# Row maxima of two dense attentions: one 128-row matmul per piece, or pairs of 64-row matmuls on the halves of the array

## The chip, the cores and the metric

One Trainium2 chip, and of it one core. The metric is the device time of one execution of the whole kernel, in microseconds (us); lower is better.

## The reference

Two transformer layers over 2048 latent tokens (width 1024) and a prefix of 256 context tokens. Each layer runs a modulated RMS norm, one input projection, two attentions, a gate, one output projection and a residual. The change touches the two *dense* attentions, mixer A of layer 0 (8 query heads, 2 key heads) and mixer C of layer 1 (4 heads, two maps each):

```python
def gqa_attend(q5, k, v):
    sc = jnp.einsum('bqkgd,bskd->bkgqs', q5, k).astype(jnp.float32) * SCALE
    p = jax.nn.softmax(sc, axis=-1).astype(v.dtype)
    return jnp.einsum('bkgqs,bskd->bqkgd', p, v)

def diff_attend(q, k, v, lam):
    sc = jnp.einsum('bqhmd,bkhmd->bhmqk', q, k).astype(jnp.float32) * SCALE
    p = jax.nn.softmax(sc, axis=-1)
    a = (p[:, :, 0] - lam * p[:, :, 1]).astype(v.dtype)
    return jnp.einsum('bhqk,bkhe->bqhe', a, v)
```

Heads are 64 wide, and all 2048 + 256 = 2304 keys are seen by each latent query. A softmax needs some number near the row's maximum, which is taken off before the exponential; any such number gives the same quotient.

## The kernel before

Every fp32 operand of an attention is kept as two fp16 halves, high and low. In DRAM, `qk` holds for each head 128 rows: rows 0 to 63 are the high half of the 64 channels, rows 64 to 127 the low half. `dense_kv` (line 1129) loads for a head `KH`, 128 rows by 2304 keys, with the high half of the keys *twice* (rows 0 to 63 and again 64 to 127), and `KL`, 65 rows, the low half and a row of constants.

`r_phase` (line 807) runs a dense attention. A unit is one head (or one map of one head) for 256 queries; each of the two attentions has 64 units. For the unit two ahead of the current one, the generator `r_front` (line 743) does the following:

- loads `Qt` (128 rows: high over low half of the queries) and `Q2` (65 rows: the high half, and a row still to be filled), on SyncE's queue;
- for each of the two halves of the queries (`t`), and for each of five pieces of the keys (four of 512, one of 256), one matmul into a PSUM tile `pM` and one VectorE reduction of it to a maximum (`mx`, line 759). With `Qt` stationary and `KH` moving, the 128 rows add up (high + low half of q) times the high half of k;
- takes the maximum over the five (`m`), writes its negative into `Z`, and brings it by a small matmul (`pM<-idh,Z`) into the last row of `Q2`.

Per unit these are 8 matmuls of 512 columns and 2 of 256, so 1024 and 256 in all. There are two `pM` buffers. For the current unit, `r_scores` (line 773) computes the scores transposed (`pS`), exponentiates on ScalarE (`Pm`), splits into `H` (ScalarE) and `L` (GpSimd), and `r_values` (line 793) multiplies by the values into `pO`. The output projection (`out_pair`, line 867; tiles `yT`, `wo`, `pX`) is fed in between as filler.

The generator is stepped a few times after each of the unit's five score groups: `for _ in range((3, 3, 2, 2, 3)[g])` (line 846). That is only the order in which the program is written down. The tile framework then simulates the program and sets each engine's order by it, so what stands next to what on TensorE follows from that scheduler and not from the source alone. All matmuls and weight loads go through the helper on line 82.

The projections ahead of an attention (`pmm<-wk,hT`) are matmuls of 256 columns. Two other matmuls matter below as a measure. `mod_cols` (line 144) issues matmuls with a stationary operand of 2 columns (`pO<-macc,sel`), which the program addresses as 128 rows by 32 columns of the array, and transposes of 2 rows (line 175, `pO<-idf,m`), addressed as 32 rows by 128 columns. All other matmuls of the attention stages and projections are addressed as the whole array, 128 by 128.

Of the kernel before, what the change touches and what calls it, by code (L numbers as in the profile page):

```python
# [8 lines left out]
F32 = mybir.dt.float32  # L9
F16 = mybir.dt.float16  # L10
AF = mybir.ActivationFunctionType
ALU = mybir.AluOpType
AX = mybir.AxisListType
# [3 lines left out]
P = 128  # L17
# [18 lines left out]
class Build:  # L36
# [424 lines left out]
    def t_block(self, Q, qs, segs, parts, tiles, nadd, add, esc, out, sink=None):  # L461
# [30 lines left out]
        yield  # L492
        Q2 = self.ap.tile([65, P], F16, name="Q2", bufs=3)
        nc.gpsimd.tensor_copy(out=Q2[0:64], in_=Q[0:64, qs])
        pz = self.ptr.tile([P, 512], F32, name="ptr")
        self.mm(pz[0:65, 0:P], Z, self.idh)
        nc.vector.tensor_copy(out=Q2[64:65], in_=pz[64:65, 0:P])
        yield
        Sb = self.ap.tile([P, 896], F32, name="Sb", bufs=self.sbufs)
        a, c0 = nadd * P, 0  # L500
        for part in (tiles[:min(nadd, 4)], tiles[min(nadd, 4):]):
# [3 lines left out]
            for j, (kh, kl, v) in enumerate(part):  # L505
                o = T[:, j * P:(j + 1) * P]
                self.mm(o, kh, Q[:, qs], True, False)
                self.mm(o, kl, Q2, False, True)
            w = len(part) * P
# [233 lines left out]
    def r_front(self, l, unit, qb, KH):  # L743

        nc = self.nc
        Qt = self.qp.tile([P, 256], F16, name="Qt")
        Q2 = self.qp.tile([65, 256], F16, name="Q2")
        nc.sync.dma_start(out=Qt, in_=self.qk[l][unit, :, qb * 256:(qb + 1) * 256])
        nc.sync.dma_start(out=Q2[0:64], in_=self.qk[l][unit, 0:64, qb * 256:(qb + 1) * 256])
        self.Qcur = (Qt, Q2)  # L750
        yield
        Zs = []
        for t in range(2):
            mx = self.smf.tile([P, 5], F32, name="mx")
            for j in range(5):
                c, n = j * 512, min(512, NTOK - j * 512)
                ps = self.pM.tile([P, 512], F32, name="pM")
                self.mm(ps[:, :n], Qt[:, t * P:(t + 1) * P], KH[:, c:c + n])
                nc.vector.tensor_reduce(out=mx[:, j:j + 1], in_=ps[:, :n], op=ALU.max, axis=AX.X)  # L759
                yield  # L760
            m = self.smf.tile([P, 1], F32, name="m")
            nc.vector.tensor_reduce(out=m, in_=mx, op=ALU.max, axis=AX.X)
            Z = self.Z[self.zi % 4]
            self.zi += 1
            nc.vector.tensor_scalar(out=Z[:, 64:65], in0=m, scalar1=-1.0 / T15, scalar2=None, op0=ALU.mult)
            Zs.append(Z)
        yield
        pz = self.pM.tile([P, 512], F32, name="pM")
        for t in range(2):
            self.mm(pz[0:65, t * P:(t + 1) * P], Zs[t], self.idh)  # L770
        nc.vector.tensor_copy(out=Q2[64:65], in_=pz[64:65, 0:256])
# [35 lines left out]
    def r_phase(self, units, front, back, finish, d, fillers):  # L807


        pend, Qs = [], []  # L810
        self.late, self.pxi = False, 0
        def first():
            e = self.early if d == 128 else self.earlyA
            return self.tc.high_priority(offset=e) if e else ExitStack()
        with first():
            for u in units[:2]:
                for _ in front(u):
                    pass
                Qs.append(self.Qcur)
        credit = [0.0] * len(fillers)  # L820

        def values():
            u, g, args, V = pend.pop(0)
            if g == 0:
                o = self.pO.tile([P, 512], F32, name="pO")
                self.Ov = o.rearrange("p (t x) -> p t x", t=2)
            self.r_values(*args, self.Ov, V, d)
            if g == 4:
                with self.tc.high_priority(offset=self.boost):
                    finish(u, self.Ov)  # L830
        for n, u in enumerate(units):
            Q = Qs.pop(0)
            f = iter(())
            self.late = n + 2 >= len(units)
            if n + 2 < len(units):
                f = front(units[n + 2])
                next(f)
                Qs.append(self.Qcur)
            KH, KL, V, esc = back(u)
            for g in range(5):  # L840
                if n == 0:
                    with first():
                        args = self.r_scores(g, Q, KH, KL, esc)
                else:
                    args = self.r_scores(g, Q, KH, KL, esc)
                for _ in range((3, 3, 2, 2, 3)[g]):
                    next(f, None)
                for i, (filler, rate) in enumerate(fillers):
                    credit[i] += rate(n)
                    while credit[i] >= 1.0:  # L850
                        credit[i] -= 1.0
                        filler.step()
                if len(pend) == self.lag:
                    values()
                pend.append((u, g, args, V))
        while pend:
            values()
# [731 lines left out]
```

## Time and profile before

| | us |
|---|---|
| median of 3 runs (lowest, highest) | 3759.36 (3756.82, 3761.03) |
| the profiled execution | 3757.87 |
| its span in the profile | 3756.1 |

The profiled execution is 1.5 us under the median, and 1.8 us longer than its span. Busy time by engine: TensorE (PE) 3596.3 us, VectorE (DVE) 2622.6, ScalarE (ACT) 2453.2, GpSimd (POOL) 2331.9.

How to read what follows: a view of the trace gives for each instruction its start and its duration. Matmuls are pipelined, so a matmul's duration (start to the last result) is longer than the distance to the next one's start. What the array gives to a matmul is that distance. A shape such as `128*128 128x256` reads: stationary operand of 128 rows by 128 columns, moving operand of 128 rows by 256 columns.

### The profile page before, as it was taken

The page shows a single profiled execution, that of the slowest core. Times are in us where ns is not written, and L with a number is a line of the kernel's source. Part 1 is how long each engine was busy: PE and PEld are TensorE (multiplying, and loading weights), DVE is VectorE, ACT ScalarE, POOL GpSimd, SP SyncE. Part 2 cuts the span into 40 slices and gives each one's busy share as a digit, 9 for nine tenths or more (in the row PEclk, how much of TensorE's full clock was granted, in tenths as well). Part 3 has the DMA queues.
Part 4 walks back from the last instruction along what each step waited for, and adds up shares of the span by engine and source line. Part 5 has one row for each costly group of instructions (what it writes and reads, how often), then busy time and mean ns, then how long its engine had stood idle before and what let it go on. Part 6 is the DMA issues. An engine that isn't in the chain of part 4 may idle for free. (4 is left out here: it accounts for less than half of the span.)

```text
span 3756.1 us, 104444 instructions
## 1 busy us (share of the span) xinstructions
PE 3596.3 (96%) x43146; PEld 2986.7 (80%) x43146; DVE 2622.6 (70%) x6646; ACT 2453.2 (65%) x4155; POOL 2331.9 (62%) x1822
## 2 busy tenths in 40 slices
PE   8889999989989999999989999999989999999998
PEld 5668988878976777777768999899878888888775
DVE  5757779898567666667666988767565656665666
ACT  5315656556668887778864666666567777776665
POOL 3204456666458888888864445435358878877785
PEclk9989999999999999999999999999999999999999
DMA  7673332223261111111133221312351211111322
GB/s 236 181 200 86 86 88 80 69 73 92 72 201 54 36 65 32 49 48 49 38 121 104 66 61 58 92 58 75 112 173 30 79 47 56 62 37 52 106 92 103
DMA packets 331972, 321.08 MB, mean 85 GB/s; under 512 B 84262, under 2 KB 283750, under 8 KB 330982
## 3 DMA queue, kind: packets, MB, share of 16 engines
q1 hardware_dynamic: 331494, 314.40, 27.7%
q8 instruction: 337, 5.52, 0.6%
q14 instruction: 141, 1.16, 0.1%
HBM read 207.43 MB, written 106.90 MB: 84 GB/s over the span
## 5 line engine op out<-in xcount | busy, mean ns | idle before, releaser
L790 POOL TENSOR_TENSOR L<-Pm,H 128x1024 f16<-128x1024 f32 (+1 forms) x640 | 1240.9, 1959 | 284.2 <-ACT H L788 207.3
L82 PE MATMUL pmm<-wk,hT 128*128 128x256 f16 x10848 | 1356.9, 275 | 21.1 <-POOL hT L277 7.2
L82 PEld LDWEIGHTS <-hT 128*128 128x128 f16 x10848 | 1026.9, 98 | 164.1 <-issue 21.8
L759 DVE TENSOR_REDUCE mx<-pM 128x1 f32<-128x512 f32 (+1 forms) x1280 | 785.7, 633 | 505.6 <-PE pM L82 496.4
L82 PE MATMUL pO<-V,H 128*128 128x65 f16 (+3 forms) x9216 | 781.0, 206 | 3.4 <-DVE ya L1267 1.8
L82 PEld LDWEIGHTS <-H 128*128 128x128 f16 x9216 | 641.5, 98 | 97.5 <-DVE ya L1267 5.2
L82 PE MATMUL pO<-V,L 128*128 128x65 f16 (+1 forms) x4608 | 707.9, 209 | 6.2 <-POOL L L790 5.8
L521 POOL TENSOR_TENSOR Pl<-Sb,Ph 128x640 f16<-128x640 f32 (+4 forms) x288 | 435.8, 1513 | 433.4 <-ACT Ph L520 260.6
L788 ACT CAST H<-Pm 128x1024 f16<-128x1024 f32 (+1 forms) x640 | 602.7, 959 | 11.8 <-PE pO L82 1.9
L82 PE MATMUL pS<-Qt,KH 128*128 128x256 f16 x2304 | 557.4, 273 | 6.2 <-ACT Pm L785 3.8
L82 PE MATMUL pS<-Q,KL 65*128 65x256 f16 x2304 | 548.1, 273 | 0.0
L82 PEld LDWEIGHTS <-L 128*128 128x128 f16 x4608 | 441.3, 97 | 51.0 <-POOL L L790 10.9
L82 PE MATMUL pM<-KH,Qt 128*128 128x512 f16 (+1 forms) x1280 | 446.5, 358 | 19.5 <-DVE mx L759 14.0
L785 ACT ACTIVATE Pm<-pS,esc_c 128x1024 f32<-128x1024 f32 (+1 forms) x320 | 323.0, 1025 | 203.8 <-PE pS L82 186.1
L82 PEld LDWEIGHTS <-KL 65*128 65x128 f16 x3824 | 371.5, 98 | 69.3 <-issue 15.7
L785 ACT ACTIVATE Pm<-pS,esc_a 128x1024 f32<-128x1024 f32 (+1 forms) x320 | 324.2, 1026 | 147.0 <-PE pS L82 109.6
L82 PE MATMUL pX<-wo,yT 128*128 128x512 f16 x1488 | 390.5, 381 | 2.0 <-ACT yT L897 1.3
L82 PEld LDWEIGHTS <-KH 128*128 128x128 f16 x2304 | 226.5, 98 | 60.7 <-issue 8.3
L82 PEld LDWEIGHTS <-yT 128*128 128x128 f16 x1632 | 154.3, 98 | 135.0 <-ACT yT L897 5.7
L520 ACT CAST Ph<-Sb 128x640 f16<-128x640 f32 (+4 forms) x288 | 220.0, 764 | 43.2 <-PE pO L82 35.0
L82 PE MATMUL pT<-Q,K 128*128 128x128 f16 x1520 | 230.7, 220 | 9.9 <-ACT Sb L516 5.0
L82 PE MATMUL pT<-Q,KL 65*128 65x128 f16 x1520 | 211.5, 220 | 0.0
(299 smaller groups left out, 5758.8 us busy)
## 6 DMA issues: line engine op xcount, KB each, us to landing
qk<-qkst SPq DMA_DIRECT2D x104, 256.0 KB, 2.3
wmod<-w_mod SPq DMA_DIRECT2D x24, 1024.0 KB, 9.1
xo<-x SPq DMA_DIRECT2D x48, 512.0 KB, 3.5
xt<-x SPq DMA_DIRECT2D x34, 512.0 KB, 4.8
G<-zz SPq DMA_DIRECT2D x68, 256.0 KB, 2.5
x<-xo SPq DMA_DIRECT2D x34, 512.0 KB, 3.3
wst<-w_in_even SPq DMA_DIRECT2D x13, 1024.0 KB, 5.5
wst<-w_in_odd SPq DMA_DIRECT2D x13, 1024.0 KB, 5.4
```

What stands on the lines that cost most here:

```text
L82: return self.nc.tensor.matmul(out=out, lhsT=l, rhs=r, start=s, stop=e, skip_group_check=skip)
L520: nc.scalar.copy(out=H[:, :n * P], in_=Sb[:, :n * P])
L521: nc.gpsimd.tensor_tensor(out=L[:, :n * P], in0=Sb[:, :n * P], in1=H[:, :n * P], op=ALU.subtract)
L759: nc.vector.tensor_reduce(out=mx[:, j:j + 1], in_=ps[:, :n], op=ALU.max, axis=AX.X)
L785: nc.scalar.activation(out=Pm[:, :n], in_=S[:, :n], func=AF.Exp, scale=esc[0], bias=LNP)
L788: nc.scalar.copy(out=H[:, :n], in_=Pm[:, :n])
L790: eng.tensor_tensor(out=L[:, :n], in0=Pm[:, :n], in1=H[:, :n], op=ALU.subtract)
```

## The change

The maxima are taken over the product of the high halves alone, 64 rows instead of 128. Two pieces form a pair: the first uses `Qt[0:64]` with `KH[0:64]`, the second uses a further tile `Qd`, into whose rows 64 to 127 the high half of the queries is loaded once more, with `KH[64:128]`. The two are thus addressed to the upper and lower 64 rows of the array (64 by 128 each) and written into the two `pM` buffers; then come the two reductions. The number of matmuls, their columns and the reductions stay; each unit gets one more DMA. The generator has fewer steps, so it is stepped (1, 1, 1, 1, 2) times.

```diff
@@ r_front
         Qt = self.qp.tile([P, 256], F16, name="Qt")
         Q2 = self.qp.tile([65, 256], F16, name="Q2")
+        Qd = self.qp.tile([P, 256], F16, name="Qd")
         nc.sync.dma_start(out=Qt, in_=self.qk[l][unit, :, qb * 256:(qb + 1) * 256])
+        nc.sync.dma_start(out=Qd[64:128], in_=self.qk[l][unit, 0:64, qb * 256:(qb + 1) * 256])
         nc.sync.dma_start(out=Q2[0:64], in_=self.qk[l][unit, 0:64, qb * 256:(qb + 1) * 256])
         self.Qcur = (Qt, Q2)
         yield
         Zs = []
-        for t in range(2):
-            mx = self.smf.tile([P, 5], F32, name="mx")
-            for j in range(5):
+        mxs = [self.smf.tile([P, 5], F32, name="mx") for t in range(2)]
+        for pair in (((0, 0), (0, 1)), ((0, 2), (0, 3)), ((1, 0), (1, 1)), ((1, 2), (1, 3)), ((0, 4), (1, 4))):
+            pss = []
+            for r, (t, j) in enumerate(pair):
                 c, n = j * 512, min(512, NTOK - j * 512)
                 ps = self.pM.tile([P, 512], F32, name="pM")
-                self.mm(ps[:, :n], Qt[:, t * P:(t + 1) * P], KH[:, c:c + n])
-                nc.vector.tensor_reduce(out=mx[:, j:j + 1], in_=ps[:, :n], op=ALU.max, axis=AX.X)
+                rows = slice(64 * r, 64 * r + 64)
+                self.mm(ps[:, :n], (Qt, Qd)[r][rows, t * P:(t + 1) * P], KH[rows, c:c + n])
+                pss.append((ps, n))
+            for (t, j), (ps, n) in zip(pair, pss):
+                nc.vector.tensor_reduce(out=mxs[t][:, j:j + 1], in_=ps[:, :n], op=ALU.max, axis=AX.X)
+            if pair[1] != (1, 4):
                 yield
+        for t in range(2):
+            mx = mxs[t]
             m = self.smf.tile([P, 1], F32, name="m")
...
@@ r_phase
-                for _ in range((3, 3, 2, 2, 3)[g]):
+                for _ in range((1, 1, 1, 1, 2)[g]):
                     next(f, None)
```

Where the scheduler puts these matmuls on TensorE, before, in the attention of layer 1 (`pO<-V,H` and `pO<-V,L` are the value products of the unit under way):

```order
L82 MATMUL pO<-V,H 128x129
L82 LDWEIGHTS Qt
L82 MATMUL pM<-KH_58635,Qt 128x512
L82 LDWEIGHTS H
L82 MATMUL pO<-V,H 128x128
L82 LDWEIGHTS L
L82 MATMUL pO<-V,L 128x129
L82 LDWEIGHTS Qt
L82 MATMUL pM<-KH_58635,Qt 128x512
L82 LDWEIGHTS H
L82 MATMUL pO<-V,H 128x129
```

Maxima and value products alternate, all of them over the whole array. TensorE's order with the change, in the same attention, one pair (`Qt` upper, `Qd` lower half):

```order
L82 LDWEIGHTS Qt
L82 MATMUL pM<-KH_62883,Qt 128x256
L82 LDWEIGHTS H
L82 MATMUL pO<-V,H 128x128
L82 LDWEIGHTS L
L82 MATMUL pO<-V,L 128x129
L82 LDWEIGHTS H
L82 MATMUL pO<-V,H 128x129
L82 LDWEIGHTS Qd
L82 MATMUL pM<-KH_62883,Qd 128x256
L82 LDWEIGHTS H
L82 MATMUL pO<-V,H 128x128
```

The two of a pair are still apart, with whole-array matmuls between them. One of the few places of TensorE's order with the change where they do stand together, near the start of the same attention (`pmm<-wk,hT` is the projection before it):

```order
L82 MATMUL pmm<-wk,hT_36138 128x256
L82 MATMUL pX<-idf,mod_81 128x128
L82 LDWEIGHTS Qt
L82 MATMUL pM<-KH_51176,Qt 128x512
L82 LDWEIGHTS Qd
L82 MATMUL pM<-KH_51176,Qd 128x512
L82 LDWEIGHTS hT_36266
L82 MATMUL pmm<-wk,hT_36266 128x256
```

Here the array is turned to 64 rows once for two matmuls. On SyncE's queue (`Q_...` is `Q2`, `y_98` an output of the attention), with the change:

```order
L749 DMA Qt<-qk_91 128x256
L751 DMA Q_62127<-qk_91 64x256
L750 DMA Qd<-qk_91 64x256
L749 DMA Qt<-qk_91 128x256
L751 DMA Q_62375<-qk_91 64x256
L750 DMA Qd<-qk_91 64x256
L1495 DMA y_98<-yc 128x2x128
```

A third load stands with the two that each unit had before.

## Rows read from the trace of the kernel before

**Rows 1.** The page, part 1: busy time of the engines.

```profile
PE 3596.3 (96%) x43146; PEld 2986.7 (80%) x43146; DVE 2622.6 (70%) x6646; ACT 2453.2 (65%) x4155; POOL 2331.9 (62%) x1822
```

**Rows 2.** Windows, dense attentions A and C (columns in the first line).

```profile
core 0: us, PE busy (x) PEld busy (x) DVE busy (x) ACT busy (x) POOL busy (x), PEclk, DMA share, GB/s
1063.00:1900.00 837.00, 814.60 (x11045) 617.06 (x11046) 573.26 (x1344) 665.57 (x765) 680.48 (x373) 1.00 0.18 59
2730.00:3680.00 950.00, 934.72 (x10554) 759.00 (x10552) 595.37 (x1319) 675.86 (x902) 741.02 (x463) 1.00 0.23 72
```

**Rows 3.** Waits of PE in attention A: total us, times, longest.

```profile
PE pM L82 <- DVE mx L759: 12.6, 17, 1.8
PE pM L82 <- DMA KH<-qk: 2.7, 1, 2.7
PE pS L82 <- ACT Pm L785: 2.6, 2, 2.3
PE pO L82 <- POOL L L790: 2.3, 3, 1.1
```

**Rows 4.** Waits of PE in attention C: total us, times, longest.

```profile
PE pO L82 <- POOL L L790: 3.6, 5, 1.7
PE ptr L82 <- DVE ssw L1308: 3.5, 1, 3.5
PE pM L82 <- DVE mx L759: 3.3, 8, 0.6
```

**Rows 5.** Lines by form, PE: maxima matmuls (busy, mean ns; idle before, releasers).

```profile
L82 PE MATMUL pM<-KH,Qt 128*128 128x512 f16 x1024 | 380.2, 379 | 15.0 <-DVE mx L759 9.6 <-DMA KH<-qk 2.7 <-DVE am L880 1.5
...
L82 PE MATMUL pM<-KH,Qt 128*128 128x256 f16 x256 | 69.6, 272 | 4.5 <-DVE mx L759 4.4
```

**Rows 6.** Timeline of PE, 3103.47 to 3103.95: start, us, instruction, count.

```profile
3103.41 0.28 PE L82 MATMUL pO<-V,H 128*128 128x129 f16 x2
3103.52 0.38 PE L82 MATMUL pM<-KH,Qt 128*128 128x512 f16 x1
3103.74 0.22 PE L82 MATMUL pO<-V,L 128*128 128x129 f16 x1
```

**Rows 7.** Timeline of PE, 259.4 to 261.1: 128x32 tiles between whole-array matmuls.

```profile
259.15 0.82 PE L82 MATMUL pmm<-wk,hT 128*128 128x256 f16 x6
259.89 1.03 PE L82 MATMUL pO<-macc,sel 128*2 128x256 f32 x4
260.85 0.50 PE L82 MATMUL pmm<-wk,hT 128*128 128x256 f16 x3
```

**Rows 8.** Timeline of PE, 151.8 to 152.6: 32x128 tiles between whole-array matmuls.

```profile
151.53 0.60 PE L82 MATMUL pmm<-wk,hT 128*128 128x256 f16 x4
152.07 0.28 PE L175 MATMUL pO<-idf,m 2*128 2x2 f32 x2
152.28 0.50 PE L82 MATMUL pmm<-wk,hT 128*128 128x256 f16 x3
```

**Rows 9.** Timeline of PE, 2000.0 to 2001.3: fp32 between fp16, all whole-array.

```profile
1999.87 0.49 PE L82 MATMUL pmm<-wk,hT 128*128 128x256 f16 x3
2000.20 1.04 PE L262 MATMUL pT<-idf,xt 128*128 128x128 f32 x8
2001.07 0.49 PE L82 MATMUL pmm<-wk,hT 128*128 128x256 f16 x3
```

**Rows 10.** The page, part 5: a weight load, mean ns of one.

```profile
L82 PEld LDWEIGHTS <-H 128*128 128x128 f16 x9216 | 641.5, 98 | 97.5 <-DVE ya L1267 5.2
```

**Rows 11.** Lines by form, DVE: the maxima.

```profile
L759 DVE TENSOR_REDUCE mx<-pM 128x1 f32<-128x512 f32 x1024 | 689.9, 687 | 464.1 <-PE pM L82 455.8 <-PE pO L82 3.0
...
L759 DVE TENSOR_REDUCE mx<-pM 128x1 f32<-128x256 f32 x256 | 106.9, 418 | 41.5 <-PE pM L82 40.6
```

**Rows 12.** DMA issues: count, KB each, us to landing (`Q` is `Q2`).

```profile
Qt<-qk SPq DMA_DIRECT2D x128, 64.0 KB, 1.9
...
Q<-qk SPq DMA_DIRECT2D x128, 32.0 KB, 2.1
```

**Rows 13.** Timeline of SyncE's queue, 3000 to 3030: two units' query loads.

```profile
3003.82 0.32 SPq L748 DMA_DIRECT2D Qt<-qk  x1
3004.24 0.45 SPq L749 DMA_DIRECT2D Q<-qk  x1
3017.27 0.32 SPq L748 DMA_DIRECT2D Qt<-qk  x1
```

## The prediction

> **What bounds the kernel now.** I read the busy shares first: TensorE is busy for 3596.3 of 3756.1 us, the next engine for 2622.6 [rows 1]. A share over the whole span can hide a stage with another limit, so I read the two stretches that the change touches: the dense attentions hold TensorE for 814.60 of 837 us and 934.72 of 950 us, with no other engine over 742 [rows 2]. Then what TensorE waits for there: the longest totals are 12.6 us (17 times) for the maxima's buffers and a few of 2 to 4 us [rows 3, 4]; with the entries too small to show, the two lists come to about 38 us of 1787. So in both stretches TensorE is the bound, its order is full, and whatever lengthens or shortens it goes nearly whole into the end. The granted clock is 1.00 in both [rows 2], although waits of up to 1.8 us and more occur [rows 3], so I take it as unchanged.
>
> What a matmul costs is the distance to the next start, not its duration. A maximum's matmul starts at 3103.52 and the next instruction at 3103.74, so 512 columns take 0.215 us, of a shown duration of 0.38 [rows 6]. Six projections of 256 columns take 0.82 us, the last lasting 0.27: 0.109 each [rows 7]. The maxima therefore hold the array for 1024 × 0.215 + 256 × 0.109 = 248 us [rows 5], of which perfect pairs would give half back.
>
> **What the scheduler makes of it.** I count in the listing of TensorE's order with the change. Of the 640 pairs only 29 stand as an unbroken `Qt`, `Qd`. Counting also a `Qd` followed by the next pair's `Qt`, there are 66 neighbourings of two 64-row matmuls (40 of two of 512 columns, 26 whose second has 256). All others stand between whole-array matmuls. The 1280 matmuls form 1214 unbroken stretches (1153 single ones, 56 twos, 5 threes; 601 in attention A, 613 in C), so the array is turned from 128 rows to 64 and back 1214 times, 2428 turns.
>
> **What a turn costs.** No 64-row matmul shows in the attentions of the trace, but two other partial tilings do. Four matmuls of 128 rows by 32 columns stand between projections: the sixth projection starts at 259.15 + 5 × 0.109 = 259.70, the first matmul after the four at 260.85, which is 1.15 us [rows 7]. Without a loss it would be one slot of 0.109 and four of 0.215 (1.03 for four, the last lasting 0.38), so 0.97. The visit costs 0.19 us: 259.89 − 259.70 − 0.109 = 0.08 to 0.09 going in, about 0.10 coming back. Two transposes on 32 rows by 128 columns cost the same going in: the fourth projection starts at 151.86, the transpose at 152.07, 0.10 over the slot [rows 8]; the way back is cheaper there, 0.21 for two tiny matmuls spaced by about 0.084 (0.28 for two, the last lasting 0.20), so 0.04 over. That neither the type nor the weight's source does this is seen where eight fp32 transposes over the whole array stand between fp16 projections: third projection at 2000.09, transpose at 2000.20, one slot; eighth at 2000.96, projection at 2001.07, one slot [rows 9]. So it is the tile's size, and the array waits for work in flight to leave before it is turned. The Trainium skill, page TensorEngine Tiling, Key Properties, says that changing the tiling mode, and not merely the tile, drains TensorE. The rows agree with about 0.1 us a turn; the same page's Theoretical Speedup allows up to twice the speed for 64 rows of contraction, and by that alone the sum would be 124 us less instead of the figure below.
>
> **The sum.**
> - *Turns.* 1214 visits × 0.20 us = **+243 us** (0.19 from rows 7, and 0.01 because the first whole-array slot after a return reads slightly longer: three projections 0.50 against 0.49 in rows 9). Bounds: the cheap way back of rows 8 makes 0.135 a visit, +164. Rows 7 went in with a weight load of 2 columns only; should a whole load of 0.098 us [rows 10] lie open as well, 0.30 a visit, +364. I take 0.20, since rows 7 have long matmuls with 256 columns, nearest to ours.
> - *Columns.* The 64-row matmuls stream as many columns as before: 0. Where two stand together they can run side by side: 40 × 0.215 + 26 × 0.109 = **−11 us**; 0 if they do not.
> - *Waits that shrink.* Other engines' work per unit does not grow, and TensorE comes later by 0.2 us ten times a unit; a turn also hides in a wait it falls into. Of the 38 us I take half, **−19 us** (bounds 0 and −38).
> - *Maxima on VectorE.* Still 1024 of 687 ns and 256 of 418 ns [rows 11], with two buffers; hidden behind TensorE, as VectorE has over 260 us to spare in each stretch [rows 2]. A pair claims both buffers at once; if that doubled the waits for them (12.6 + 3.3 us) it would cost +16. I take 0.
> - *The extra load.* 128 DMAs like `Q2`'s: 32 KB, 2.1 us to landing [rows 12], 0.45 us on SyncE's queue [rows 13]. Behind it there queue `Q2`, the outputs and the projection's loads, each moved by 0.45 us in the 13 us from one unit's loads to the next [rows 13]; the maxima that read it are two units away. Cost 0; were `KH`'s one wait of 2.7 us [rows 3] repeated at each attention's start, +5.
> - *The generator's steps.* Six steps still finish a unit's front within the unit: 0.
>
> Together +243 − 11 − 19 = **+213 us**. On the profiled execution's 3757.9 us this gives **3971 us**; the median of the runs stands 1.5 us higher, which I leave inside the range. The extremes are 3757.9 + 164 − 11 − 38 = 3873 and 3757.9 + 364 + 16 + 5 = 4143.
>
> **Rivals.**
> 1. *Half tiles are turned to without a drain* (not slower). Then only the neighbourings count: 3757.9 − 11 = 3747, or 3758 if they run in turn. For it: no row shows 64 rows with fp16. Against it: both partial tilings that the trace has, by rows and by columns, pay on entry. It decides when a visit costs less than 11 / 1214 = 0.009 us; the rows show twenty times that. Chance 0.05.
> 2. *The halves overlap although others stand between them* (faster): a 64-row matmul runs beside its whole-array neighbours or waits for its partner, and all 640 pairs are had: 512 × 0.215 + 128 × 0.109 = 124 us less, 3634. Against it: in every row above starts follow the listing one by one. With pairs but with turns it would be 3757.9 − 124 + 640 × 0.20 = 3762, so even standing together they would gain nothing. Chance 0.03 for the first form. The Trainium skill, page TensorE: Matmul & The Clock Gate, "What overlaps and what doesn't", has matmuls in strict order; rows 6 to 9 agree.
> 3. *A turn is dearer*: the weight load lies open each time, 0.30 us a visit, and pairs that take both `pM` buffers add their waits: up to 4143, from about 0.25 a visit on. For it: rows 7 never loaded 128 columns on entry. Against: coming back, a whole load did come and 0.10 was all. Chance 0.06.
>
> **How the numbers follow.** The forecast, turns of 0.16 to 0.23 us each visit, has 0.86. Its own spread is 1214 × 0.16 − 11 − 38 = +145 to 1214 × 0.23 = +279, so about 3903 to 4037; I give **3905 to 4035**, leaving out rivals 1 and 2, the dear part of 3, and a little of either end. A difference of 0.2% (7.5 us) is about what a measurement can tell. Faster by more: 0.05 (rival 2 and nearly half of 1). Within: 0.03. Slower by more: 0.92.
>
> **What would show it.** In the profile after, a single 64-row matmul of 512 columns should have about 0.31 us to the next start instead of 0.215, and the matmul ahead of it about 0.09 more than its slot; TensorE's shape reads 64*128. Attention A should grow by some 110 us and C by as much, the projections by nothing; VectorE's total for the maxima stays near 797 us, and its wait for `pM` grows. In the 66 neighbourings the second should start almost with the first. The forecast is wrong if starts around lone 64-row matmuls keep 0.215 and 0.056 (rival 1), if the two of a separated pair overlap (rival 2), or if the growth sits in waits for `mx` or `Qd` rather than next to the 64-row matmuls.

## The result, and the profile after

The changed kernel takes 3979.15 us (median of 4 runs, 3973.41 to 3982.30) against 3760.2 us before: a ratio of 1.0581, 95% interval 1.0568 to 1.0593. That is 219 us slower; 3971 was forecast. The profiled execution took 3973.41 us, with a span of 3971.6.

The page of the changed kernel, part 1, answers to [rows 1]:

```profile
PE 3829.7 (96%) x43146; PEld 2963.4 (75%) x43146; DVE 2631.6 (66%) x6646; ACT 2456.3 (62%) x4155; POOL 2337.2 (59%) x1822
```

TensorE has the same 43146 matmuls and is busy for 233 us more; the other engines stay within 9 us. The lines by form of the changed kernel, for the maxima, answer to [rows 5]:

```profile
L82 PE MATMUL pM<-KH,Qt 64*128 64x512 f16 x512 | 198.1, 387 | 5.2 <-DMA KH<-qk 3.9 <-DVE Q L780 0.7 <-DVE mx L765 0.5
L82 PE MATMUL pM<-KH,Qd 64*128 64x512 f16 x512 | 198.1, 387 | 5.4 <-DVE mx L765 4.8 <-DMA Qd<-qk 0.5
```

One such matmul lasts 387 ns where it lasted 379, so the loss is not in the matmul's own duration. It lies beside it. The timeline of PE in the changed kernel, around a lone 64-row matmul in attention C (start, us, instruction, count), answers to [rows 6]:

```profile
3208.58 0.22 PE L82 MATMUL pO<-V,H 128*128 128x129 f16 x1
3208.73 0.39 PE L82 MATMUL pM<-KH,Qd 64*128 64x512 f16 x1
3209.05 0.23 PE L82 MATMUL pO<-V,H 128*128 128x128 f16 x1
3209.12 0.22 PE L82 MATMUL pO<-V,L 128*128 128x129 f16 x1
```

From the value product to the 64-row matmul there are 0.15 us, where a value product's slot is 0.057; from that matmul to the next product 0.32, where the slot is 0.215. The slot of the product behind is 0.067 (the row rounds it to 0.07), 0.01 too long. The profile shows no wait at these places. I read the gap as the array being turned; the experiments below test that. Where two of different halves stand together, the changed kernel's timeline in attention A shows:

```profile
1245.37 0.20 PE L82 MATMUL pO<-V,L 128*128 128x65 f16 x1
1245.49 0.39 PE L82 MATMUL pM<-KH,Qt 64*128 64x512 f16 x1
1245.50 0.39 PE L82 MATMUL pM<-KH,Qd 64*128 64x512 f16 x1
1245.81 0.39 PE L82 MATMUL pX<-wo,yT 128*128 128x512 f16 x1
```

Both start within 0.01 us and are followed 0.32 us later: two for the price of one, with one visit.

To see how general this is, I took for every matmul of the trace the distance to the next start, less the median distance of its shape (for a 64-row one, of the 128-row shape with as many columns). I call this difference its excess. Ahead of the 1214 stretches of 64-row matmuls the median excess is 0.096 us, behind them 0.104, and 0.010 in the slot after. Together a visit costs **0.21 us**, whatever the neighbour's shape is.

### The profile page after: what moved, and what is told of

It reads as the page before. It is cut to its first block, busy times and chain, and to the rows that moved or that the text cites. A ratio compares the mean times of both kernels' runs of the same rounds, so it can differ in the third digit from the quotient of the medians.

```text
span 3971.6 us, 104677 instructions
## 1 busy us (share of the span) xinstructions
PE 3829.7 (96%) x43146; PEld 2963.4 (75%) x43146; DVE 2631.6 (66%) x6646; ACT 2456.3 (62%) x4155; POOL 2337.2 (59%) x1822
## 5 line engine op out<-in xcount | busy, mean ns | idle before, releaser
L765 DVE TENSOR_REDUCE mx<-pM 128x1 f32<-128x512 f32 (+1 forms) x1280 | 804.6, 636 | 729.3 <-PE pM L82 717.1
L82 PE MATMUL pO<-V,H 128*128 128x65 f16 (+3 forms) x9216 | 769.9, 207 | 0.7 <-DVE o L1470 0.4
L82 PE MATMUL pO<-V,L 128*128 128x65 f16 (+1 forms) x4608 | 699.5, 209 | 6.0 <-POOL L L799 5.8
L82 PEld LDWEIGHTS <-H 128*128 128x128 f16 x9216 | 619.0, 98 | 115.2 <-issue 51.7
L82 PEld LDWEIGHTS <-yT 128*128 128x128 f16 x1632 | 133.2, 98 | 165.2 <-issue 62.0
L82 PE MATMUL pM<-KH,Qd 64*128 64x512 f16 (+1 forms) x640 | 234.0, 366 | 7.6 <-DVE mx L765 6.6
L82 PE MATMUL pM<-KH,Qt 64*128 64x512 f16 (+1 forms) x640 | 234.0, 366 | 5.2 <-DMA KH<-qk 3.9
```

The lines of the kernel that those rows point to most:

```text
L82: return self.nc.tensor.matmul(out=out, lhsT=l, rhs=r, start=s, stop=e, skip_group_check=skip)
L765: nc.vector.tensor_reduce(out=mxs[t][:, j:j + 1], in_=ps[:, :n], op=ALU.max, axis=AX.X)
```

## The experiments

The theory is that a visit to the half-array setting costs 0.21 us, and that the order makes 1214 of them. The rivals put the time on what else the change brought: 64-row matmuls as such, the pairing and its order, the further load, the new steps.

**One matmul alone, without pairs.** The kernel before, with the upper half of both operands only.

```diff
-                self.mm(ps[:, :n], Qt[:, t * P:(t + 1) * P], KH[:, c:c + n])
+                self.mm(ps[:, :n], Qt[0:64, t * P:(t + 1) * P], KH[0:64, c:c + n])
```

> The kernel before with one edit: the maxima's matmuls take rows 0 to 63 of Qt and KH; no pairs, no further load, steps as before. TensorE's order has 1213 stretches of 64-row matmuls, none on the other half. Theory (each visit to the half-array setting costs 0.21 us, as the changed kernel's profile reads): 3760 + 1213 x 0.21 = 4015, less some 20 us of waits that shrink, so 3985 to 4015, a little over the changed kernel since nothing overlaps. Rival (the pairing, the extra load or the new steps cost the time): about 3760.

Measured: 3983.5 us, ratio 1.0593 (1.0577 to 1.0609), 1.5 us under the stated range. No pair, no `Qd`, no new step, and the whole loss is there.

**One row more.** The same with `Qt[0:65]` and `KH[0:65]`, so that one channel of the queries' low half is in the maxima. 65 rows are addressed to the whole array.

> As lone64, but with rows 0 to 64 of Qt and KH, one row more, which is addressed to the whole array. Theory: no visit, 3750 to 3770. Rival (a matmul of fewer than 128 rows is itself slower, or frees nothing else): about what lone64 gives.

Measured: 3766.97 us, ratio 1.0017 (1.0008 to 1.0026). Adding one row takes 217 us off. The two timelines of PE, first with 64 rows:

```profile
3209.47 0.22 PE L82 MATMUL pO<-V,H 128*128 128x129 f16 x1
3209.63 0.39 PE L82 MATMUL pM<-KH,Qt 64*128 64x512 f16 x1
3209.95 0.23 PE L82 MATMUL pO<-V,H 128*128 128x128 f16 x1
```

and with 65:

```profile
3201.53 0.22 PE L82 MATMUL pO<-V,L 128*128 128x129 f16 x1
3201.59 0.38 PE L82 MATMUL pM<-KH,Qt 65*128 65x512 f16 x1
3201.81 0.28 PE L82 MATMUL pO<-V,H 128*128 128x129 f16 x2
```

Distances of 0.16 and 0.32 us become 0.06 and 0.22. The scheduler's order differs between the two in places, but TensorE has nearly as many stretches of maxima in either (1213 with 64 rows, 1207 with 65). So it is the setting of the array, not the small number of rows at work, the maxima's value or the schedule.

**The pairs, the load and the steps, on the whole array.** The changed kernel, with one edit:

```diff
-                self.mm(ps[:, :n], (Qt, Qd)[r][rows, t * P:(t + 1) * P], KH[rows, c:c + n])
+                self.mm(ps[:, :n], Qt[:, t * P:(t + 1) * P], KH[:, c:c + n])
```

> The changed kernel with one edit: both matmuls of a pair take all 128 rows of Qt and KH, as before the change; pairs, the load of Qd (which nothing reads) and the steps stay. Theory: no visit, 3750 to 3775. Rival (pairing, load or steps cost the time): 3960 to 3990.

Measured: 3772.52 us, ratio 1.0029 (1.0018 to 1.0039). Order, load and steps cost 12 us together, not 219. Which of the three costs them was not tried.

**The pairs kept together.** In the changed kernel each half of a pair waits for a buffer of its own, which I took for the reason that they stand apart. With one tile of two banks both become ready at once:

```diff
-                ps = self.pM.tile([P, 512], F32, name="pM")
+                if r == 0:
+                    two = self.pM.tile([P, 1024], F32, name="pM")
+                ps = two[:, r * 512:(r + 1) * 512]
...
-            q[n] = self.pool(s, f"p{n}{tag}", 2 if n == "M" else 1, PSUM)
+            q[n] = self.pool(s, f"p{n}{tag}", 1, PSUM)
```

> The changed kernel with the two PSUM buffers of a pair made one tile of two banks, so that both matmuls become ready at once: in TensorE's order 638 of 640 pairs stand together, 641 stretches. Theory: 641 x 0.21 = 135 us of visits against 638 overlaps worth 124 us: 3750 to 3780, near the kernel before. Rival (an overlapping pair costs no turn, or turns are only dear when a half stands alone): about 3640. Rival (the order, load or steps): about 3970.

Measured: 3884.99 us, ratio 1.0329 (1.0314 to 1.0344). None of the three forecasts was met. The trace says that the pairs did what was asked: 638 second halves start within 0.02 us of the first, and by the same account as above the overlaps give back 122 us, while 641 visits at 0.21 take 135. What grows are waits. The page's waits of PE over the whole run of this kernel (total us, times, longest), first entries:

```profile
PE pO L82 <- POOL L L801: 36.1, 67, 2.5
PE pM L82 <- DVE mx L767: 18.8, 25, 2.0
PE pS L82 <- ACT Pm L796: 17.1, 33, 1.3
```

**Are those waits the buffer's or the visits'?** The last kernel with 128 rows for both of a pair, no other edit. (The scheduler set TensorE's order anew; it agrees with that of 'together' in 40849 of 43146 places.)

> The run 'together' with one edit: both matmuls of a pair take all 128 rows, as before the change; the one tile of two banks stays, the pairs stand together, nothing turns and nothing overlaps. In the trace of 'together' 641 visits and 638 overlaps nearly cancel (135 against 122 us), and some 110 us of waits around buffers are new. Theory (those waits come from the one tile, which both reductions must leave before the next pair starts): 3850 to 3880. Rival (the waits come with the turns, so that a visit costs far more than 0.21 us): 3760 to 3785.

Measured: 3894.04 us, ratio 1.0348 (1.033 to 1.0365), above the stated 3850 to 3880 but far from the rival's 3785. With no visit and no overlap the time is 9 us longer than with both (the intervals of the two ratios overlap). Its waits of PE:

```profile
PE pO L82 <- POOL L L801: 37.2, 68, 4.7
PE pM L82 <- DVE mx L767: 23.7, 35, 2.0
PE pM L82 <- DVE Z L776: 18.1, 17, 4.9
```

They are much the same kind and as long, without any turn. The list of the kernel before has no wait of `pM` for `Z`, and for the other two

```profile
PE pM L82 <- DVE mx L759: 15.9, 25, 1.8
PE pO L82 <- POOL L L790: 5.8, 8, 1.7
```

So the one tile, which both reductions must leave before the next pair or `Z`'s matmul can enter, and the order that came with it cost about 130 us together. The waits for the tile itself (`mx` and `Z`) are 26 us of this in the list; the 31 us more for GpSimd's `L` are no wait for the tile, and why they grew is not shown. On equal buffers, pairs that stand together are no slower than whole-array matmuls (9 us faster by the medians, which the intervals do not settle); by visits and overlaps alone they should be 13 us slower.

**Longer visits.** If a visit has a fixed price, it should hold more. Four matmuls of 512 columns go into one tile of four banks (two on each half of the array), reduced 1024 columns at a time. The banks come from the scores, whose two buffers shrink from two banks to one, with an exponential per 512 columns. The generator has fewer steps and is stepped (1, 0, 1, 1, 1) times:

```diff
+        for visit in (((0, 0), (0, 1), (0, 2), (0, 3)), ((1, 0), (1, 1), (1, 2), (1, 3)), ((0, 4), (1, 4))):
+            big = self.pM.tile([P, 2048], F32, name="pM")
+            for i, (t, j) in enumerate(visit):
+                c, n = j * 512, min(512, NTOK - j * 512)
+                rows = slice(64 * (i % 2), 64 * (i % 2) + 64)
+                self.mm(big[:, i * 512:i * 512 + n], (Qt, Qd)[i % 2][rows, t * P:(t + 1) * P], KH[rows, c:c + n])
...
-        S = self.pSs[1].tile([P, 1024], F32, name="pS")
+        for h in range(0, len(kts), 2):
+            self.pSs.reverse()
+            S = self.pSs[1].tile([P, 512], F32, name="pS")
```

> Longer visits: four matmuls of 512 columns at a time into one tile of four banks, reduced by two reductions of 1024; the scores' two buffers shrink to one bank each, with an exponential per 512. In TensorE's order 389 stretches, 249 of them of four. Theory: 389 x 0.21 = 82 us of visits against 122 us of overlaps, 40 us less than the same buffers with 128 rows (the run 'quads128'); against the kernel before 3720 if the buffers cost nothing, up to 3840 if they cost what they seem to in 'together'. Rival (visits cost more the more they hold): at or above 'quads128'.

> The run 'quads' with one edit: all four matmuls take 128 rows, so no visit and no overlap; buffers and order stay. Theory: 40 us above 'quads'; against the kernel before between 3760 and 3880, whatever the one tile and the smaller score buffers cost. Rival: at or below 'quads'.

Measured: 3769.69 us, ratio 1.0022 (1.0013 to 1.0032), and with 128 rows in the same buffers 3829.41 us, ratio 1.0175 (1.016 to 1.019). The half-array version wins by 60 us, where 40 were expected (TensorE's order agrees in 41572 of 43146 places). The timeline of PE in 'quads' shows one visit:

```profile
3213.87 0.22 PE L82 MATMUL pO<-V,L 128*128 128x129 f16 x1
3214.03 0.39 PE L82 MATMUL pM<-KH,Qt 64*128 64x512 f16 x1
3214.03 0.39 PE L82 MATMUL pM<-KH,Qd 64*128 64x512 f16 x1
3214.26 0.38 PE L82 MATMUL pM<-KH,Qt 64*128 64x512 f16 x1
3214.26 0.38 PE L82 MATMUL pM<-KH,Qd 64*128 64x512 f16 x1
3214.57 0.29 PE L82 MATMUL pO<-V,H 128*128 128x129 f16 x2
```

Four matmuls of 512 columns take 0.70 us from the product ahead to the product behind. On the whole array they would take 0.057 + 4 × 0.215 = 0.92.

**The ends of the attentions.** 'quads' seemed to lose time where its large tile meets the stages around it. The projection's last matmuls got a quarter of one shared tile each, and attention C other banks:

```diff
-            return self.pM.tile([P, 2048], F32, name="pM")[:, 0:512]
+            if self.lateM is None:
+                self.lateM = self.pM.tile([P, 2048], F32, name="pM")
+            self.lateq = (self.lateq + 1) % 4
+            return self.lateM[:, self.lateq * 512:(self.lateq + 1) * 512]
...
-        for n in (("M", "S0", "S1"), ("S1", "M", "S0"))[tag == "C"]:
+        for n in (("M", "S0", "S1"), ("S0", "S1", "M"))[tag == "C"]:
```

> The run 'quads' with two edits of its buffers: the projection's last matmuls share one tile of four banks by quarters, instead of taking the whole tile each, and in attention C the tile of four banks lies on banks that the projection ahead frees early. 413 stretches. Theory: 413 x 0.21 = 87 us of visits, 122 us of overlaps; 'quads' lost some 20 us at the ends of the two attentions, so 3740 to 3765, under the kernel before. Rival (what 'quads' gives back lies in the middle of the attentions, in the smaller score buffers): as 'quads', 3770.

Measured: 3771.95 us, ratio 1.0039 (1.0025 to 1.0054): a miss, and as slow as 'quads', as its rival said. What 'quads' gives back in attention C is not settled by this.

**Quads in attention A alone.** The kernel before, with the functions of 'quads' where the attention is A, and its own where it is C:

```diff
+    def r_front(self, l, *a):
+        return (self.front_128 if l else self.front_quads)(l, *a)
+
+    def r_scores(self, *a):
+        return (self.scores_quads if self.quads else self.scores_128)(*a)
...
-            q[n] = self.pool(s, f"p{n}{tag}", 2 if n == "M" else 1, PSUM)
+            q[n] = self.pool(s, f"p{n}{tag}", 2 if n == "M" and tag == "C" else 1, PSUM)
+        self.quads = tag == "A"
```

> The kernel before, with the quads of the run 'quads' (tile of four banks, one-bank score buffers) in attention A alone; attention C as before, with 128 rows. About 197 stretches of 64-row matmuls. Theory: in 'quads' the projection after A begins at 1931 instead of 1939, so A gains some 8 us over the kernel before, and C gives 20 back; here 3745 to 3757, under the kernel before. Rival (A's 8 us are lost again in the stages behind, or come from the order): 3757 to 3770.

Measured: 3752.03 us, ratio 0.9975 (0.9965 to 0.9986). By the medians it beats the changed kernel by far and the one before by 7 us. The tile view of `pM` for the starts in attention A (count, durations min/median/max, first and last start) has in this kernel

```profile
L82 PE MATMUL pM<-KH,Qt x320: 266/376/631, 1077.8 to 1868.6; 64*128 64x512 f16 x128, 64*128 64x256 f16 x32
```

and in the kernel before

```profile
L82 PE MATMUL pM<-KH,Qt x640: 269/378/632, 1063.7 to 1881.2; 128*128 128x512 f16 x128, 128*128 128x256 f16 x32
```

The maxima start 14 us later and end 13 us earlier. The profiled execution does not show the gain: its span is only 1.7 us shorter (3754.4 against 3756.1), and the projection behind A begins at 1938.1 us where it began at 1939.4, not at the 1931 that the expectation took from 'quads'. Nor does any run have these buffers in A with 128 rows. So what the 7 us come from is open; what two pairs a visit are worth is read from 'quads' against 'quads128'.

## Why the prediction was right

*The bound.* TensorE was the bound and stayed it: 233 us more of busy time came out as 215.5 us more of span (3971.6 − 3756.1). The two attentions carry it, as forecast. The same view as just shown, for both attentions of the changed kernel:

```profile
L82 PE MATMUL pM<-KH,Qd x320: 266/386/605, 1063.2 to 1992.0; 64*128 64x512 f16 x128, 64*128 64x256 f16 x32
...
L82 PE MATMUL pM<-KH,Qt x320: 266/386/387, 2811.1 to 3899.1; 64*128 64x512 f16 x128, 64*128 64x256 f16 x32
```

From the first to the last maximum A took 818 us (above) and takes 930 (`Qt`'s first start is 1061.9); C took 968 (2708.8 to 3677.0) and takes 1088. That is 113 and 120 us more, against "some 110 us and C by as much". The stage between them has not grown (828 us from A's last maximum to C's first before, 819 after).

*The order.* 1214 stretches and 66 neighbourings were read from the listing, and the trace has the 1214 as listed. Of the 66, 50 start together and give back 8.6 us, where 11 were forecast; in the other 16 the second waited.

*The price of a turn.* This was the weak point, since no 64-row fp16 matmul showed in the trace. 0.20 us a visit was taken from 128x32 tiles [rows 7]; 0.21 was measured, +255 us instead of +243. The cheap way back that the prediction read from the 2-column transposes [rows 8] holds for neither 512 nor 256 columns (0.104 and 0.103 us behind lone ones). Rival 3's 0.30 is out by its size. Nor do 0.096 and 0.104 us stand for a weight load of 0.098 us [rows 10] that lies open, as the near numbers might suggest. The timeline of weight loads (PEld) at the lone matmul of the result, in the changed kernel:

```profile
3208.52 0.10 PEld L82 LDWEIGHTS <-H 128*128 128x128 f16 x1
3208.73 0.09 PEld L82 LDWEIGHTS <-Qd 64*128 64x128 f16 x1
3209.05 0.10 PEld L82 LDWEIGHTS <-H 128*128 128x128 f16 x1 [0.23 <-issue]
```

The first load starts 0.06 us ahead of its matmul at 3208.58, under the one before. The other two start with theirs, at 3208.73 and 3209.05 (0.004 us ahead, by the medians of the lone 64-row matmuls). So in the gap neither a matmul nor a load starts: the load, too, waits until the turn is over. Rival 1, turning without a drain, falls with 'lone64'; rival 2, overlap across other matmuls, falls with the timelines, where no start departs from the listing. The Trainium skill's TensorEngine Tiling, Key Properties, has a change of mode drain TensorE. The trace agrees: at every one of the 1214 stretches the first 64-row matmul starts at least 0.091 us after its slot, and the maxima with 65 rows show no such gap. That what fills the gap is work leaving the array is the reading of the Trainium skill and of the prediction; the trace shows only the gap.

*Waits that shrink.* 19 us were taken. By the account over all starts, excesses away from the visits fell by 57 us, and about 26 of these reappear as waits at the visits, so some 30 net. The sum then reads 255 − 9 − 30 = 216, which is the growth of the span. That the forecast of 3971 lies 2 us from the profiled execution is thus partly luck: the turns were taken 12 us too low, the overlaps 2 us too high and the shrinking waits 11 us too low, and these nearly cancel.

*What was costed at nothing.* VectorE's maxima are 1024 of 690 ns and 256 of 422, in all 805 us against 797 [rows 11]; PE's wait for `mx` is 7.1 us, less than before. The further load lands in 2.1 us as `Q2`'s does, and makes PE wait for 0.5 us in all. 'pairs128' puts these, the order and the steps at 12 us together in a kernel without visits, where the forecast had 0.

*One claim of the prediction needs mending.* It said pairs that stand together would gain nothing (3762 by its sum). Visits and overlaps do nearly cancel, 135 against 122 us, but the kernel that keeps them together pays 130 us for the buffer that does it, which the sum had not considered; and on equal buffers it was no slower (9 us faster by the medians), where 13 us more were expected. In the account over all starts, of the profiled executions, the some 20 us between these and 13 of the 20 by which 'quads' beat its own sum are waits: with visits at 0.21 us and overlaps taken out, the excesses add up to 356 us in 'together' and 379 in 'together128', and to 293 in 'quads' and 306 in 'quads128'. What shortens the waits is not shown by a run.

## What to carry to other kernels

Splitting the array is a setting that is paid for on each entry and each return, so count the entries in the *scheduled* order, not the pairs in the source. Here a visit of one pair of 512 columns breaks even (0.21 us against 0.215 saved) and a visit of two pairs wins (60 us on equal buffers); a lone half tile lost its 0.21 us each time. Two matmuls stayed neighbours once they became ready together, which one tile over both banks brought about, but the price of that tile should be measured with the old matmuls in it. And where fewer than 128 rows are wanted without company, 65 rows can be cheaper than 64: here by 217 us over 1213 visits.

## What the runs showed of the hardware

- A visit from the whole array to 64 rows by 128 columns and back costs 0.096 + 0.104 + 0.010 us in the changed kernel, 'lone64' and 'together'. The way in is 0.093 to 0.098 us behind 64, 128, 256 or 512 columns.
- The first slot after a turn is 0.010 us longer, on the way in as on the way back. Behind a lone matmul it is part of the 0.104. In the visits of four of 'quads' and 'quads_A' it shows by itself: the second pair starts 0.226 us after the first, where the slot is 0.215, and the way back is 0.093. The visit costs 0.21 there too.
- Two 64-row matmuls on different halves start 0.003 to 0.004 us apart and share one slot. Two on the *same* half ('lone64') follow each other at 0.226 us, one slot with these 0.010, and share nothing.
- The clock stayed: the windows of the two attentions in the changed kernel, from the first to the last maximum, read 0.99 and 1.00 of the higher level (2.4 GHz) in the third column from the end, although the array is turned 1.2 times a microsecond (2428 turns in 2019 us).

```profile
1062.00:1992.00 930.00, 916.92 (x10851) 602.59 (x10850) 567.17 (x1330) 654.81 (x749) 669.80 (x367) 0.99 0.17 54
2811.00:3900.00 1089.00, 1075.23 (x10740) 756.58 (x10739) 609.74 (x1339) 685.63 (x915) 748.53 (x466) 1.00 0.23 72
```
